# Output projection's weights split in the LRU stage, and eight of its row tiles written beside retention and GLA

## The chip, the cores and the metric

The kernel runs on one core of a Trainium2 chip, as one program with one launch. The metric is device time in microseconds (us), the median of three runs. The engines are named as in the profile: PE (TensorE, matmuls), DVE (VectorE), ACT (ScalarE), POOL (GpSimd) and SP (SyncE, which here issues nearly all DMAs). Each engine works through its own list of instructions in order, and waits at an instruction until the semaphores that it needs have come.

## The reference

One layer: four token mixers side by side on the input projection (retention, RWKV-7, RG-LRU, GLA), an output projection with a residual, and a mixture of experts in which each expert chooses its tokens. Everything is float32; the sequence has 2048 tokens of width 1024.

```python
h = _rmsnorm(x, norm_mix[l])
proj = jnp.einsum('btd,dc->btc', h, w_in[l]).astype(jnp.float32)
...
o_ret = _retention_group(rq, rk, rv, rg, positions, ret_log_decay[l], ret_gn[l])
o_rwkv = _rwkv7_group(wr, wk, wv, wxw, wxa, wxg, ...)
o_lru = _rglru_group(lx, lgate, lru_conv_w[l], ...)
o_gla = _gla_group(gq, gk, gv, gog, gxa, ...)
mixed = jnp.concatenate([o_ret, o_rwkv, o_lru, o_gla], axis=-1).astype(x.dtype)
x = x + jnp.einsum('btc,cd->btd', mixed, w_out[l])
x = x + _expert_choice_ffn(_rmsnorm(x, norm_ffn[l]), router_w[l], router_b[l], exp_w_gate[l], exp_w_up[l], exp_w_down[l])
return _rmsnorm(x, norm_final)
```

The change concerns the line with `w_out` alone: what is computed stays the same.

## The kernel before, in words

Every large matmul is done as three, on operands split into a high and a low part (`split`: ACT copies the source into the high part in a rounded format, L43, and DVE or POOL subtracts it from the source for the low part, L44; `mm3` then multiplies high by high, high by low and low by high, L129).

The program goes through these stages. (1) The input projection, with the LRU group (`lru`, once per half of its channels) written beside it: PE multiplies projections while ACT, DVE and POOL work on LRU's 128x2048 tiles. (2) The rest of the projection, beside the first half of RWKV (`stage_a`, `rwkv_a`). (3) Three streams woven by weights of their own: the second half of RWKV with what follows it (`rwkv_rest`), retention, and GLA. (4) The output projection of the row tiles that are left. (5) `top_k` of the router, and the experts.

The order of the instructions on each engine is set by a scheduler, from the order in which the program is written, the priorities of the weave, and its own estimates of time. Buffers come from pools, stacked on two sides of the on-chip memory; a pool that is closed gives its place to later ones, which then wait for the last user of that place. Two such waits matter here. LRU's pool (`lr`) gives its place to the pools of `rwkv_a`, so the first RWKV load (`ld`) waits until LRU's result (`mx<-lr_i`, L1067) has been stored. And the pools of the output projection in stage 4 (`wom`, `wo2`) lie where retention and GLA had theirs.

The output projection takes row tiles of 128 tokens. `out_weights` loads `w_out` in four pieces of 128x2048 (1 MB each) into `wo_st`, on a pool of two buffers (`wst`), and splits each into `wo_hi` and `wo_lo`; the low parts of pieces 0 and 2 are DVE's, those of 1 and 3 POOL's. `out_proj` loads the mixers' outputs of a tile from DRAM (`wo_mx<-mx`), splits them into `wo_mh` and `wo_ml`, loads the residual (`wo_x`), multiplies (48 matmuls of 128x512 for each tile), adds, and makes the router's logits. Tiles 4 to 7 (`EARLY = 4`) are written at the end of `rwkv_rest`, one tile at a time with one buffer for `wo_x`, on the right-hand pools; the other twelve, in stage 4, two at a time with two buffers.

Retention works tile by tile with one buffer for its input (`rt_ld`, L933): transposes (L938), scores (L952), outputs (L960, L963), the state's update (L909), and only then the next load. After four tiles it, as GLA, writes a block of 512 tokens to `mx` (`gated_out`, L983 to L985). SP's list holds all these loads and stores in one order.

Of the kernel before, what the change touches and what calls it, by code (L numbers as in the profile page):

```python
# [6 lines left out]
F32 = mybir.dt.float32  # L7
F32R = mybir.dt.float32r
# [9 lines left out]
P = 128  # L18
T = 2048
D = 1024  # L20
KD = D // P
# [19 lines left out]
def split(g, hi, lo, src, pool=False):  # L41

    g.nc.scalar.activation(out=hi, in_=src, func=AF.Copy)  # L43
    (g.nc.gpsimd if pool else g.nc.vector).tensor_tensor(out=lo, in0=src, in1=hi.bitcast(F32), op=OP.subtract)  # L44
# [191 lines left out]
def drain(gen):  # L236
    for _ in gen:
        pass
# [1010 lines left out]
CAP = 2 * T // NE  # L1249
HROW = D + NE  # L1250
LATE = 5
EARLY = 4
WA, WP = 84, 92
JOIN = 3
WR, WG = 100, 68
# [9 lines left out]
    c["fs_tok"] = np.stack([np.broadcast_to(np.arange(NB, dtype=f), (128, NB)), np.broadcast_to(i[:, None].astype(f), (128, NB))], 2).copy()  # L1265


def out_weights(g):
    nc, d, big = g.nc, g.d, g.wo
    whi = big.tile([P, KD, D], F32R, name="wo_hi")  # L1270
    wlo = big.tile([P, KD, D], F32R, name="wo_lo")
    nf = big.tile([P, D], F32, name="wo_nf")
    rw = big.tile([P, KD, 32], F32, name="wo_rw")
    nc.gpsimd.memset(rw, 0.0)
    g.consts(big, "fs_e")
    rb = big.tile([P, NE], F32, name="wo_rb")
    g.wout = whi, wlo, nf, rw, rb
    for n in range(4):
        st = g.wst.tile([P, KD, 256], F32, name="wo_st")
        s = slice(256 * n, 256 * n + 256)  # L1280
        nc.sync.dma_start(out=st, in_=d["w_out"][0, :, s].rearrange("(k p) c -> p k c", p=P))
        split(g, whi[:, :, s], wlo[:, :, s], st, n % 2)
        if n == 3:
            nc.sync.dma_start(out=nf, in_=d["norm_ffn"].broadcast_to([P, D]))
            nc.sync.dma_start(out=rw[:, :, 0:NE], in_=d["router_w"][0].rearrange("(k p) e -> p k e", p=P))
            nft = big.tile([P, KD], F32, name="wo_nft")
            nc.sync.dma_start(out=nft, in_=d["norm_ffn"][0].rearrange("(k p) -> p k", p=P), allow_slow_non_contiguous=True)
            nc.vector.tensor_tensor(out=rw, in0=rw, in1=nft[:, :, None].broadcast_to([P, KD, 32]), op=OP.mult)
            nc.sync.dma_start(out=rb, in_=d["router_b"].broadcast_to([P, NE]))
        yield  # L1290
# [375 lines left out]
def program(tc, d, out):  # L1666
    g = Ctx()
    g.tc, g.nc, g.d = tc, tc.nc, d
    nc = g.nc
# [11 lines left out]
    def pool(es, name, bufs, **kw):  # L1681
        return es.enter_context(tc.tile_pool(name=name, bufs=bufs, **kw))
# [9 lines left out]
    with ExitStack() as es:  # L1692
# [4 lines left out]
        dt = g.dr.tile  # L1697
# [3 lines left out]
        g.rw_tl = dt([4, 64, 1024], F32, name="rw_tl")  # L1701
        g.ysp = [dt([NB, P, 256], F32, name=f"ysp{i}") for i in range(2)]
        g.rw_dg, g.rw_ti = (dt([4, P, 1024], F32, name=n) for n in ("rw_dg", "rw_ti"))
        g.bonus = dt([P, 2, T], F32, name="bonus")
        g.gl_sp = dt([NB // GB, P, 4 * GP], F32, name="gl_sp")
        g.mx = dt([P, KD, T], F32, name="mx")
# [7 lines left out]
        with ExitStack() as es1:  # L1714
# [17 lines left out]
            with ExitStack() as es2:  # L1732
                g.lp = pool(es2, "lr", 1)
                g.stream = 0
                lru(g, 0)
                lru(g, 1)
                g.stream = 1
                drain(second)
            g.ap, g.ip = pool(es1, "ra", 1), pool(es1, "ri", 1)
# [19 lines left out]
        right = es.enter_context(ExitStack())  # L1759

        def rwkv_rest():
            g.fin = pool(right, "fin", 1, side="right")
            with ExitStack() as es1:
                g.fp, g.bp = pool(es1, "rf", 1, side="right"), pool(es1, "rb", 2, side="right")
                g.rj = pool(es1, "rj", 1, side="right")
                g.mp, g.ep = pool(es1, "rm", 4, side="right"), pool(es1, "re", 4, side="right")
                rwkv_b_buffers(g)
                yield from rwkv_b(g)
            g.wo = pool(right, "wo", 1, side="right")
            with ExitStack() as es1:  # L1770
                g.wst = pool(es1, "wst", 2, side="right")
                yield from out_weights(g)
            p1, p2 = pool(right, "we", 2, side="right"), pool(right, "we2", 1, side="right")
            yield from out_proj(g, p1, p2, range(4, 4 + EARLY), 1, 0, 1)
        with ExitStack() as es1:
            g.rp, g.rw2 = pool(es1, "rt", 1), pool(es1, "rt2", 1)
            g.gb, g.gw, g.sh = pool(es1, "gl", 1), pool(es1, "gl2", 1), pool(es1, "sh", 1)
            consts(g.rp, "rt_zt rt_inv")
            consts(g.gb, "gl_m gl_hq")
            rest = streamed(g, 0, rwkv_rest())  # L1780
            next(rest)
            g.stream = 1
            ret_tables(g)
            drain(weave((rest, WR), (streamed(g, 1, retention(g)), 56), (streamed(g, 2, gla(g)), WG)))
        g.stream = 0
        with ExitStack() as es1:
            p1, p2 = pool(es1, "wom", 2), pool(es1, "wo2", 2)
            drain(out_proj(g, p1, p2, [*range(4 + EARLY, 12, 2), 0, 2, 12, 14], 2, 1, 2))
        right.close()
# [36 lines left out]
```

## Time and profile before

| what | value |
|---|---|
| runs of the kernel before | 2861.94 us median (2858.56, 2861.94, 2866.71) |
| the profiled execution | 2858.58 us, span 2856.6 us |
| busy share of the span | PE 91%, weight loads 81%, DVE 61%, ACT 49%, POOL 25% |
| DMA | 538.40 MB, mean 188 GB/s |

The span is the time from the first to the last instruction in the profile; the execution's own time is 2.0 us longer. Times in views are us from the span's start. A row of a timeline gives start, duration, engine, line, operation, output and inputs, and in brackets the idle time of the engine just before, with what ended it.

### The profile page before, as it was taken

What the parts mean: (1) busy time and instruction counts of PE and PEld (TensorE: products, weight loads), DVE (VectorE), ACT (ScalarE), POOL (GpSimd) and SP (SyncE); (2) the same over time, 40 slices, a digit from 0 to 9 for tenths busy, and PEclk for the clock granted to TensorE, in tenths of its full rate; (3) what the DMA queues carried; (4) which work ended last, traced back from release to release, by engine and by line L of the source; (5) the groups of instructions that cost most, each with busy time, mean ns of one, the idle gap of its engine ahead of it and who ended that gap; (6) DMA issues with size and microseconds to landing.
All of it is one profiled execution on the core that took longest, in us unless ns stands there. A gap on an engine that the chain in (4) does not pass through costs nothing.

```text
span 2856.6 us, 47428 instructions
## 1 busy us (share of the span) xinstructions
PE 2594.7 (91%) x18433; PEld 2321.6 (81%) x18433; DVE 1746.1 (61%) x3415; ACT 1392.3 (49%) x2348; POOL 711.5 (25%) x771
## 2 busy tenths in 40 slices
PE   6989998989888888886979859999999999999997
PEld 5866787768767777774767659999999999999987
DVE  4454567766887667788443475555555555566564
ACT  4366555435434676555533334444444444455453
POOL 0011115443524454347433200000000000000121
PEclk9999999999988889997989979999999999999999
DMA  8735554675446544446344346666666666789873
GB/s 304 278 101 190 182 164 151 203 231 166 136 122 177 161 153 148 145 127 190 107 143 171 127 147 206 205 206 205 206 205 205 205 206 206 228 289 298 266 238 140
DMA packets 474015, 538.40 MB, mean 188 GB/s; under 512 B 129952, under 2 KB 411584, under 8 KB 473024
## 3 DMA queue, kind: packets, MB, share of 16 engines
q1 hardware_dynamic: 461984, 492.12, 53.3%
q0 software_dynamic: 11808, 43.26, 5.8%
q8 instruction: 145, 2.38, 0.3%
q14 instruction: 78, 0.64, 0.1%
HBM read 392.17 MB, written 145.23 MB: 188 GB/s over the span
## 4 chain that ended last, share of the span: by engine, by line
PE 53%; DVE 5%; DMA 4%; ACT 3%; issue 2%; POOL 1%; SPq 0%; POOLq 0%; ACTq 0%; DVEq 0%
PE bank L129 43%; DMA rt_ld<-tm 1%; PE bank L656 1%; PE bank L1500 1%; PE bank L639 1%; DMA fn_x<-acc,x_idx 1%; PE bank L628 1%; PE bank L672 1%; PE bank L1481 1%; PE bank L648 1%; DVE tk_j L1395 0%; PE bank L1217 0%; PE bank L1323 0%; PE bank L960 0%; PE bank L952 0%
## 5 line engine op out<-in xcount | busy, mean ns | idle before, releaser
L44 DVE TENSOR_TENSOR x_wl<-x_st,x_wh 128x2048 fp32r<-128x2048 f32 x192 | 439.5, 2292 | 306.3 <-ACT x_wh L43 305.9
L129 PE MATMUL bank<-x_xh,x_wh 128*128 128x256 f32 x2048 | 580.2, 285 | 2.9 <-ACT x_wh L43 2.8
L129 PE MATMUL bank<-x_xl,x_wh 128*128 128x256 f32 x2048 | 577.4, 283 | 0.0
L129 PE MATMUL bank<-x_xh,x_wl 128*128 128x256 f32 x2048 | 572.2, 283 | 1.1 <-DVE x_wl L44 1.1
L43 ACT ACTIVATE x_wh<-x_st 128x2048 fp32r<-128x2048 f32 x192 | 367.0, 1913 | 106.7 <-PE bank L129 96.6
L129 PEld LDWEIGHTS bank<-x_xh,x_wh 128*128 128x128 f32 x2048 | 393.2, 192 | 3.6 <-ACT x_wh L43 3.2
L129 PEld LDWEIGHTS bank<-x_xl,x_wh 128*128 128x128 f32 x2048 | 393.3, 192 | 0.0
L129 PEld LDWEIGHTS bank<-x_xh,x_wl 128*128 128x128 f32 x2048 | 389.9, 192 | 1.5 <-DVE x_wl L44 1.5
L129 PE MATMUL bank<-x_wh,x_hh 128*128 128x256 f32 x1024 | 290.1, 285 | 4.8 <-ACT x_hh L43 4.8
L129 PE MATMUL bank<-x_wl,x_hh 128*128 128x256 f32 x1024 | 291.2, 285 | 0.0
L129 PE MATMUL bank<-x_wh,x_hl 128*128 128x256 f32 x1024 | 289.8, 284 | 0.0
L1626 POOL DMA_INDIRECT acc<-x_os,x_idx x30 | 48.9, 1631 | 926.8 <-ACT x_os L1560 899.0
L129 PE MATMUL bank<-h_hi,w_hi 128*128 128x512 f32 x576 | 238.5, 417 | 20.1 <-DVE o_cm L1676 13.8
L129 PE MATMUL bank<-h_lo,w_hi 128*128 128x512 f32 x576 | 240.0, 417 | 0.0
L129 PE MATMUL bank<-h_hi,w_lo 128*128 128x512 f32 x576 | 235.6, 409 | 0.0
L129 PEld LDWEIGHTS bank<-x_wh,x_hh 128*128 128x128 f32 x1024 | 196.6, 193 | 5.0 <-ACT x_hh L43 5.0
L129 PEld LDWEIGHTS bank<-x_wl,x_hh 128*128 128x128 f32 x1024 | 197.4, 193 | 0.0
L129 PEld LDWEIGHTS bank<-x_wh,x_hl 128*128 128x128 f32 x1024 | 197.2, 193 | 0.0
L129 PE MATMUL bank<-w_hi,h_hi 128*128 128x256 f32 (+1 forms) x512 | 156.4, 306 | 14.6 <-DVE o_tm L1676 11.8
L129 PEld LDWEIGHTS bank<-h_hi,w_hi 128*128 128x128 f32 x576 | 112.5, 196 | 56.3 <-DVE o_cm L1676 16.4
L129 PE MATMUL bank<-w_lo,h_hi 128*128 128x256 f32 (+1 forms) x512 | 149.4, 292 | 0.0
L129 PE MATMUL bank<-w_hi,h_lo 128*128 128x256 f32 (+1 forms) x512 | 148.8, 291 | 0.0
(457 smaller groups left out, 5490.2 us busy)
## 6 DMA issues: line engine op xcount, KB each, us to landing
x_st<-in_exp_w_gate_dram SPq DMA_DIRECT2D x64, 1024.0 KB, 8.4
x_st<-in_exp_w_up_dram SPq DMA_DIRECT2D x64, 1024.0 KB, 8.9
x_st<-in_exp_w_down_dram SPq DMA_DIRECT2D x64, 1024.0 KB, 5.5
w_st<-in_w_in_dram SPq DMA_DIRECT2D x20, 1024.0 KB, 6.7
rw_sp<-sp SPq DMA_DIRECT2D x16, 1280.0 KB, 4.6
bld<-rw_sp SPq DMA_DIRECT2D x32, 640.0 KB, 4.1
ld<-rw_cm SPq DMA_DIRECT2D x14, 899.5 KB, 6.1
cm<-o_cm SPq DMA_DIRECT2D x40, 256.0 KB, 2.8
```

The lines of the kernel that those rows point to most:

```text
L43: g.nc.scalar.activation(out=hi, in_=src, func=AF.Copy)
L44: (g.nc.gpsimd if pool else g.nc.vector).tensor_tensor(out=lo, in0=src, in1=hi.bitcast(F32), op=OP.subtract)
L129: g.nc.tensor.matmul(out, lhsT=lhs[a][:, k, lsl], rhs=rhs[b][:, k, rsl], start=(k + i == 0 and out is outs[0]), stop=(3 * k + i == 3 * nk ...
L628: nc.tensor.matmul(pss[k][:, q * P:(q + 1) * P], lhsT=z[q][H[k]], rhs=ks, start=True, stop=True)
L639: nc.tensor.matmul(ps[:, o:o + P], lhsT=bk[q][e], rhs=rd[:, 2 * q + 1 - e], start=True, stop=True)
L648: nc.tensor.matmul(ps[:, h * P:(h + 1) * P], lhsT=ti[:, h], rhs=R[:, h], start=True, stop=True)
L656: nc.tensor.matmul(ps[:, h * 256:(h + 1) * 256], lhsT=X[:, 2 * h2 + h, :], rhs=q0[:, 2 * h2 + h].rearrange("p e c -> p (e c)"), start=True ...
L672: nc.tensor.matmul(ps[:, h, :], lhsT=E[:, h, e, :], rhs=mv[e][:, h, :], start=True, stop=True)
L1481: nc.tensor.matmul(ps[:, 2 * s:2 * s + 2], lhsT=oh[:, i, s * P:(s + 1) * P], rhs=tok[:, i], start=(i == 0), stop=(i == NB - 1))
L1500: nc.tensor.transpose(ps[:, m * CAP + s * P:m * CAP + (s + 1) * P], xs[:, s, (k + m) * P:(k + m + 1) * P], c["ident"])
L1626: g.nc.gpsimd.indirect_dma_start(out=dst, out_offset=bass.IndirectOffsetOnAxis(ap=idx[:, s:s + 1], axis=0), in_=t[:, s], in_offset=None, **kw)
```

## The change

Three edits. A new function, `out_split`, stands behind the two calls of `lru`, in their pool: in 16 pieces of 128x512 it loads `w_out`, splits each piece (ACT for the high part, DVE for the low part) and stores both parts in two new DRAM tensors, `wo_sp`. Its buffers (`wo_st`, `wo_sh`, `wo_sl`) are one of each. `out_weights` no longer splits: it loads the two parts from there, eight loads of 1 MB straight into `wo_hi` and `wo_lo`, and the pool `wst` is gone. `EARLY` goes from 4 to 8: tiles 4 to 11 are written in `rwkv_rest`, and stage 4 keeps tiles 0 to 3 and 12 to 15.

```diff
-EARLY = 4
+EARLY = 8
...
+def out_split(g):
+
+    nc = g.nc
+    for n in range(4):
+        for k in range(0, KD, 2):
+            st = g.lp.tile([P, 2, 256], F32, name="wo_st", tag="wo_st")
+            hi = g.lp.tile([P, 2, 256], F32R, name="wo_sh", tag="wo_sh")
+            lo = g.lp.tile([P, 2, 256], F32R, name="wo_sl", tag="wo_sl")
+            s = slice(256 * n, 256 * n + 256)
+            nc.sync.dma_start(out=st, in_=g.d["w_out"][0, k * P:(k + 2) * P, s].rearrange("(k p) c -> p k c", p=P))
+            split(g, hi, lo, st)
+            for t, o in zip((hi, lo), g.wo_sp):
+                nc.sync.dma_start(out=o[:, k:k + 2, s], in_=t.bitcast(F32))
...
     for n in range(4):
-        st = g.wst.tile([P, KD, 256], F32, name="wo_st")
         s = slice(256 * n, 256 * n + 256)
-        nc.sync.dma_start(out=st, in_=d["w_out"][0, :, s].rearrange("(k p) c -> p k c", p=P))
-        split(g, whi[:, :, s], wlo[:, :, s], st, n % 2)
+        for t, k in zip((whi, wlo), g.wo_sp):
+            nc.sync.dma_start(out=t[:, :, s].bitcast(F32), in_=k[:, :, s])
...
+        g.wo_sp = [dt([P, KD, D], F32, name=f"wo_sp{i}") for i in range(2)]
...
                 lru(g, 1)
+                out_split(g)
                 g.stream = 1
                 drain(second)
...
-            with ExitStack() as es1:
-                g.wst = pool(es1, "wst", 2, side="right")
-                yield from out_weights(g)
+            yield from out_weights(g)
             p1, p2 = pool(right, "we", 2, side="right"), pool(right, "we2", 1, side="right")
             yield from out_proj(g, p1, p2, range(4, 4 + EARLY), 1, 0, 1)
```

Lines of the changed kernel are 14 higher behind `out_split` (L1301 is L1315, L1309 is L1323, L1678 is L1692), and 14 to 16 lines higher further on. The scheduler's order is the same on PE from early in `rwkv_a` until shortly after RWKV's last chain; it differs in the LRU stage and behind that point.

ACT in the first half of LRU, before: sigmoids (`lr_r`, `lr_i`), a square (`lr_a`), a square root (`lr_th`), and the table loads between them.

```order
L1046 ACTIVATE lr_i<-bank,lr_gb 128x512
L1052 ACTIVATE lr_a_1133<-lr_r 128x2048
L1046 ACTIVATE lr_i<-bank,lr_gb 128x512 x2
L1046 ACTIVATE lr_r<-bank,lr_gb 128x512
L1055 ACT_TABLE_LOAD
L1055 ACTIVATE lr_th<-lr_th 128x2048
L1046 ACT_TABLE_LOAD
L1046 ACTIVATE lr_r<-bank,lr_gb 128x512 x3
```

The same place in the changed kernel:

```order
L1046 ACTIVATE lr_i<-bank,lr_gb 128x512
L43 ACTIVATE wo_sh<-wo_st 128x512
L1046 ACTIVATE lr_i<-bank,lr_gb 128x512 x2
L1052 ACTIVATE lr_a_1135<-lr_r 128x2048
L1046 ACTIVATE lr_i<-bank,lr_gb 128x512
L43 ACTIVATE wo_sh<-wo_st 128x512
L1046 ACTIVATE lr_r<-bank,lr_gb 128x512
L1055 ACT_TABLE_LOAD
L1055 ACTIVATE lr_th<-lr_th 128x2048
L1046 ACT_TABLE_LOAD
L1046 ACTIVATE lr_r<-bank,lr_gb 128x512 x2
L43 ACTIVATE wo_sh<-wo_st 128x512
```

Three of the sixteen high parts (`wo_sh`) now stand between LRU's instructions here. In all, six stand in the first half's run of sigmoids and square roots, which has one table load fewer than before, and four in the second half's; the other six stand between these runs or ahead of them.

SP behind RWKV's last chain, before: the last two loads of `w_out` (`wo_st`), then RWKV's, GLA's and retention's loads, and the first tile's `wo_mx`.

```order
L1281 DMA wo_st<-in_w_out_dram 128x8x256
L764 DMA rw_y_12854<-ysp_76 128x2x256
L769 DMA bon<-bonus 128x2x256
L1146 DMA gl_p<-gl_sp 128x1024
L1281 DMA wo_st<-in_w_out_dram 128x8x256
L1181 DMA gl_v<-tm 128x2x256
L764 DMA rw_y_12853<-ysp_75 128x2x256
L767 DMA xg<-rw_cm 128x256
L785 DMA mx<-bon 128x2x256
L1301 DMA wo_mx<-mx 128x8x128
L933 DMA rt_ld<-tm 128x768
```

The changed kernel, the end of the eight loads of the split weights (six more stand right ahead of these rows, and one retention load, of tile A below, ahead of those):

```order
L1296 DMA wo_hi<-wo_sp_79 128x8x256
L764 DMA rw_y_12936<-ysp_75 128x2x256
L1296 DMA wo_lo<-wo_sp_80 128x8x256
L767 DMA xg<-rw_cm 128x256
L1298 DMA wo_nf<-in_norm_ffn_dram 128x1024
L785 DMA mx<-bon 128x2x256
L1299 DMA wo_rw<-in_router_w_dram 128x8x16
L1301 DMA wo_nft<-in_norm_ffn_dram 128x8x1
L1303 DMA wo_rb<-in_router_b_dram 128x16
L1315 DMA wo_mx<-mx 128x8x128
L1146 DMA gl_p<-gl_sp 128x1024
L933 DMA rt_ld<-tm 128x768
```

The next retention load (of tile B), GLA's `gl_p` and RWKV's `rw_y` now stand behind 8 MB of weights.

PE at its first matmul of the output projection, before: GLA, the gate of a retention block (L983), RWKV's output (L778, L780), and then the projection.

```order
L1217 MATMUL bank<-gl_qx,gl_p 128x512
L1236 MATMUL bank<-gl_v,gl_sT 128x64 x4
L1217 MATMUL bank<-gl_qx,gl_p 128x512
L1233 MATMUL bank<-gl_sx_7412,gl_p 128x256
L1234 MATMUL bank<-gl_sx_7413,gl_p 128x256
L983 MATMUL bank<-c_ident,rt_y_10496 128x128 x8
L778 MATMUL bank<-c_ident,rw_y_12853 128x128 x4
L780 MATMUL bank<-xg,rw_g_up 128x256 x2
L129 MATMUL bank<-wo_hi,wo_mh 128x512
L129 MATMUL bank<-wo_lo,wo_mh 128x512
```

The changed kernel, from the end of retention's tile B (its last output and its state's update) to the first matmul of the projection:

```order
L960 MATMUL bank<-rt_sd_7497,rt_qs 128x128
L963 MATMUL bank<-rt_ld,rt_sT 128x64 x2
L909 MATMUL bank<-rt_ld,rt_kz 128x128 x2
L938 MATMUL bank<-c_ident,rt_a_11758 128x128 x4
L1153 MATMUL bank<-c_ident,gl_p 128x128 x2
L952 MATMUL bank<-rt_qd_7493,rt_kT 128x256 x2
L778 MATMUL bank<-c_ident,rw_y_12983 128x128 x4
L780 MATMUL bank<-xg,rw_g_up 128x256 x2
L129 MATMUL bank<-wo_hi,wo_mh 128x512
L129 MATMUL bank<-wo_lo,wo_mh 128x512
```

Ahead of the first projection matmul PE now does all of retention's tile B and the front (L938, L952) of tile C, where it had done tile A alone: 36 more matmuls (16 of tile B, 6 of tile C, GLA's 8 gate transposes, 6 small ones). At the far end, matmuls of stage 4's tiles 0 to 3 now stand between those of tiles 6 to 11, ahead of the last block of retention and GLA.

## Rows read from the trace of the kernel before

**Rows 1.** The chain that ended last, in order of time: start, us, what, count.
```profile
1446.03 9.23 DMA wo_mx<-mx
1465.29 7.68 PE bank L129 x24
1473.85 5.62 PE bank L129 x24
1627.52 2.85 DMA c_fs_iota<-in_c_fs_iota_dram
```

**Rows 2.** Windows: us; busy PE, PEld, DVE, ACT, POOL; PE clock; DMA share; GB/s.
```profile
1300.00:1350.00 50.00, 25.70 (x107) 17.60 (x107) 45.01 (x75) 25.84 (x53) 41.49 (x33) 0.66 0.50 151
1350.00:1450.00 100.00, 91.15 (x532) 72.71 (x530) 48.34 (x131) 46.82 (x109) 48.00 (x46) 0.94 0.34 114
1450.00:1475.00 25.00, 11.65 (x46) 9.48 (x47) 12.30 (x31) 7.75 (x9) 9.41 (x5) 0.61 0.47 153
1475.00:1525.00 50.00, 50.00 (x272) 39.01 (x271) 19.73 (x63) 19.23 (x34) 17.55 (x10) 1.00 0.48 170
```

**Rows 3.** Timeline of DVE and POOL, the splits of the weights.
```profile
1301.02 10.27 DVE L44 TENSOR_TENSOR wo_lo<-wo_st,wo_hi 128x2048 fp32r<-128x2048 f32 x1 [0.79 <-ACT wo_hi L43]
1320.05 2.29 DVE L44 TENSOR_TENSOR wo_lo<-wo_st,wo_hi 128x2048 fp32r<-128x2048 f32 x1
1324.40 4.61 POOL L44 TENSOR_TENSOR wo_lo<-wo_st,wo_hi 128x2048 fp32r<-128x2048 f32 x1 [0.52 <-ACT wo_hi L43]
```

**Rows 4.** Waits of PE between 1290 and 1480: us, times, longest.
```profile
PE bank L1233 <- DVE gl_t L1227: 8.2, 1, 8.2
```

**Rows 5.** Timeline of SP, loads and stores issued (start, us of issue).
```profile
1288.01 1.17 SPq L1281 DMA_DIRECT2D wo_st<-in_w_out_dram  x2
1293.48 0.52 SPq L933 DMA_DIRECT2D rt_ld<-tm  x1
1329.50 0.53 SPq L1301 DMA_DIRECT2D wo_mx<-mx  x1
```

**Rows 6.** DMAs of 1284 to 1335 (GB/s in 40 slices), and `wo_x` there and in 1380 to 1440.
```profile
GB/s 265 219 240 43 258 364 376 341 353 381 409 410 226 285 288 242 335 95 6 1 0 0 158 372 376 366 357 371 355 139 180 0 0 6 107 202 258 257 377 238
wo_x<-in_x_dram SPq DMA_DIRECT2D x1, 512.0 KB, 8.1
wo_x<-in_x_dram SPq DMA_DIRECT2D x3, 512.0 KB, 3.6
```

**Rows 7.** Timeline of SP and PE, one retention tile, and the first projection matmul.
```profile
1275.91 0.32 SPq L933 DMA_DIRECT2D rt_ld<-tm  x1
1287.32 1.10 PE L952 MATMUL bank<-rt_qd,rt_kT 128*128 128x256 f32 x4
1290.59 0.66 PE L909 MATMUL bank<-rt_ld,rt_kz 128*128 128x128 f32 x4
1352.82 0.80 PE L129 MATMUL bank<-wo_hi,wo_mh 128*128 128x512 f32 x1
```

**Rows 8.** Timeline of POOL, ACT and PE where LRU ends and `rwkv_a` begins.
```profile
288.31 1.81 POOL L1741 MEMSET bl<- 128x2048 f32 x1 [16.19 <-DMA mx<-lr_i]
297.09 0.42 ACT L356 ACTIVATE xwa<-xwa 64x256 f32<-64x256 f32 x1
299.92 1.14 PE L362 MATMUL bank<-xwa,rw_up 64*128 64x256 f32 x8
```

**Rows 9.** Rows nearest to a 128x512 piece: one tile's groups (ns), timelines (us).
```profile
L43 ACT ACTIVATE wo_mh<-wo_mx x20: 612/1040/1064, 1334.0 to 1573.4; 128x1024 fp32r<-128x1024 f32 x12, 128x512 fp32r<-128x512 f32 x8
1280.86 0.68 DVE L878 TENSOR_TENSOR rt_a<-rt_ld,rt_cs 128x512 f32<-128x512 f32 x1
168.81 1.28 ACT L1055 ACT_TABLE_LOAD   x1
252.75 2.29 DVE L1056 TENSOR_TENSOR lr_i<-lr_i,lr_th 128x2048 f32<-128x2048 f32 x1 [3.87 <-POOL lr_i L1047]
DMA to landing us min/median/max: 2.6/2.7/2.9
```

## The prediction

> **What bounds the kernel now.** I read the chain of waits in order of time first. From the experts on it is PE's matmuls without a break, so what counts is when the top-k begins: the chain meets its first load at 1627.5 [rows 1]. Ahead of that the chain enters stage 4 through a load of `mx` at 1446.0, and PE's first matmul of that stage comes at 1465.3 [rows 1]. The windows over this stretch come next. From 1475 on PE is busy all the time; in 1450 to 1475 it is busy 11.65 of 25 us, in 1350 to 1450 91.15 of 100, in 1300 to 1350 25.70 of 50 [rows 2]. So PE is the bound, with three holes of 24.3, 8.85 and 13.35 us, and the change can win what it fills of these.
>
> The first hole lies where the weights are split. DVE spends 10.27 us on one low part and 2.29 on an equal one; POOL takes 4.61 for its own [rows 3]. PE meanwhile waits 8.2 us for a GLA instruction that DVE has behind the split [rows 4]. The third hole is a change of pools: tile 8's load can only be issued when retention and GLA have left their place, and nothing else is written for PE there.
>
> **The change part by part.** The sum is made on the profiled execution: span 2856.6, own time 2858.58, which is 3.4 below the median of 2861.94.
>
> *The third hole.* By the changed order, matmuls of tiles 0 to 3 and 6 to 11 stand around the end of retention and GLA, all on weights and buffers that are there by then. PE has work while stage 4's pools change: 13.35 us go. After the hole the first 24 matmuls took 7.68 us where the next 24 took 5.62 [rows 1], and the granted clock in that window was 0.61, in the next 1.00 [rows 2]; without the idle time I take these 2.1 us as won too. Together 15.4.
>
> *The first hole, the weights.* What goes from DVE, ACT and POOL are four splits (DVE 12.6 us, POOL about 9.2 [rows 3]). What comes is a load of 8.4 MB in place of 4.2 MB. The slices of 1.3 us in which the old loads ran (the fifth to the twelfth that hold 258 to 410) have a mean of about 361 GB/s [rows 6], so 8.4 MB need 23 us. In the changed order the eight loads stand behind retention's load for tile A, which was issued at 1293.5 [rows 5], and some small transfers; I put their first byte at about 1298 and their last at 1322. The first tile's `wo_mx` is queued right behind them, where it was issued at 1329.5 before [rows 5]: the weights themselves come a few us earlier than now.
>
> That does not help PE at once, since its order now holds retention's tile B and the front of tile C ahead of the first projection matmul. Retention has one input buffer. An undisturbed tile took from the load's issue at 1275.9 to the end of L909 at 1291.25, 15.3 us, and reached L952 after 11.4 [rows 7]. So tile A ends at 1293.5 + 15.3 = 1309. Tile B's load is issued then, but stands behind the weights, `wo_mx` and `gl_p` (1 MB more, 3 us): it lands at about 1326, where it would have landed near 1313 on an empty queue, and tile B ends at 1326 + 12 = 1338. Tile C's load comes at about 1340, its L952 at 1351, and the first projection matmul at about 1353. It is at 1352.8 now [rows 7]: no gain, no loss. The gain is what PE has done by then: 36 more matmuls. Tile B from L952 to L909 is 3.9 us [rows 7]; with the transposes and the GLA gate I count 7 us for all 36. They fill a part of the first hole.
>
> *The second hole.* Tiles 4 to 7 are woven with retention and GLA as now, one tile at a time on one `wo_x` buffer. I leave the 8.85 us as they are, though the order differs; the bounds are nothing (8.85 won) and twice as much (8.85 lost, if eight tiles on one buffer stall more than four).
>
> *The LRU stage.* 16 pieces come in, each with a load, a copy on ACT, a subtraction on DVE and two stores. The nearest rows: 0.61 us for an ACT copy of 128x512, 0.68 for a DVE operation of that size on two on-chip inputs, 2.6 to 2.9 us for a 256 KB load to land [rows 9]. The DMAs (12.6 MB, 35 us at 361 GB/s) find room in a stage of 170 us; no row shows them beside this traffic, so zero is the lower bound and the pieces' own latency the upper one, below. ACT has ten copies within LRU's dense runs: 6.1 us, less one table load of 1.28 [rows 9]. On DVE most subtractions fall where it idles for POOL's product, 3.87 us in the row shown [rows 9]; two do not, 1.4. LRU's end is thus 6.2 us later, and it is what `rwkv_a` waits for: POOL's clearing of `bl` started on the landing of `mx<-lr_i` [rows 8]. PE reached L362 2.4 us after its input was ready (297.5 and 299.92 [rows 8]), and the changed order puts L362 three matmuls later, 1.2 us. Of 6.2 us some 2.6 are left, and I take 3 for the loss. From there on PE's order is as before, so a shift of 3 us is carried to the end.
>
> *SP's list.* SP waits in order. Stores of a piece stand between stores of projection results, so a late ACT copy holds those stores; PE goes on as long as the two result buffers last. I put that at 0, with the cover of one buffer (some 10 us of matmuls).
>
> *Sum.* -15.4 - 7 + 3 = -19.4. Own time 2858.6 - 19.4 = 2839; against the median 2842.5. **Forecast: 2843.**
>
> **A rule on the queue.** The 512 KB load of `wo_x` took 8.1 us to land behind the 2 MB of `wo_st`, and 3.6 later on, so transfers queued on SP's list wait for those ahead [rows 6]. The Trainium skill (DMA: Bandwidth & Descriptors, Queues, rings and completion order) says that descriptors of a queue are taken in ring order and that a transfer's semaphore write lands only after every earlier write of that DMA engine. By that rule every load of retention, GLA and RWKV behind the eight is held for their whole drain, and the trace agrees as far as these two rows go. What it gives here is rival A: the price is set by the drain, from rows.
>
> **The rivals.**
>
> *A: the 8.4 MB hold retention back, and the gain is used up.* The 361 GB/s above are those of a burst; over 1300 to 1350 only 151 GB/s were moved, and over all 40 slices about 230 [rows 2, 6]. At 230 GB/s the 8.4 MB take 36.5 us instead of 23, and the 1 MB behind them 4.5 instead of 3: tile B comes 15 us later, and so does the first projection matmul. For it: PE's order puts tiles B and C ahead of that. Against it: the low slices are those in which nothing was asked for. The gain shrinks from 22.4 to about 7, the result to -4: 2858, no difference. Chance 0.17.
>
> *B: slower, through LRU.* If each of the ten copies in LRU's runs stands at ACT's head waiting for its load, a piece costs 2.7 us to land, 0.61, and 0.68 before the buffer is free [rows 9]: 4.0 times ten is 40 us on LRU's end, with 3.6 of slack and order. The loss is 36, the sum +14: 2876. It decides against the change once LRU ends more than 26 us later (22.4 + 3.6). For it: one buffer per piece, a load behind SP's waits, ACT and PE coupled through LRU's banks. Against it: in the changed order several LRU instructions stand between two copies on ACT, 5 to 8 us by their durations, more than a load takes. Chance 0.10.
>
> *C: more of the holes is filled.* If tile B's load lands early, so that the projection starts at 1340, and half of the second hole goes as well, 13 + 4.4 us more: 2825. The first hole is 24.3 us wide, and DVE is free in it now. Chance 0.13.
>
> **How the numbers follow.** Forecast 0.60, A 0.17, B 0.10, C 0.13. The forecast's own bounds: the second hole gone or doubled (8.85 either way) and LRU's loss between 0 and 8, so 2831 to 2857. For 8 in 10 I take 2828 to 2862, which adds A and the near part of C. A change under 0.3% (8.6 us) is about what three runs of this kernel, 8 us apart, can't tell from none. Faster by more (below 2853.4): 0.73, most of the forecast and C, with a little of A. Within 0.3%: 0.17. Slower: 0.10, rival B.
>
> **What would show it right or wrong.** In the changed profile: the DVE and POOL splits of 128x2048 of `wo_st` are gone, and eight loads of `wo_hi` and `wo_lo` are issued within a few us near 1298. The first projection matmul comes at about 1356 (1353 and 3 of shift), with PE still half idle before it; behind it there is no window like 1450 to 1475, and the top-k's first load is issued at about 1608. `mx<-lr_i` of the second half lands some 6 us later, and L362 starts near 303. The prediction is wrong if LRU's end moves by more than 15 us, if tile B's load lands after 1335, or if PE idles behind the first projection matmul, for instance on the single `wo_x` buffer or because its list has a retention matmul, not yet ready, ahead of projection matmuls that are.

## The result, and the profile after

The change is slower: 2885.12 us median of 6 runs (2877.14 to 2890.19), against 2867.05 for the kernel before in the same session (6 runs, 2858.56 to 2871.09); ratio 1.0065, 95% interval 1.0049 to 1.0080, some 18 us. The forecast was 2843, with a range to 2862. The profiled executions stand further apart (spans 2883.7 and 2856.6), because the one of before took 2858.58, as long as the fastest of its six. So totals below go by ratios of medians, and profiles serve to find places. In rows, SPq and ACTq are DMAs that SP or ACT issues.

Timeline of SP in the changed kernel: retention's load of tile A, part of the loads behind it, tile B's and tile C's loads, and the first of the top-k's loads (start, us of issue):

```profile
1321.38 0.46 SPq L933 DMA_DIRECT2D rt_ld<-tm  x1
...
1322.84 0.52 SPq L1296 DMA_DIRECT2D wo_hi<-wo_sp  x1
1323.42 0.75 SPq L1296 DMA_DIRECT2D wo_lo<-wo_sp  x1
1324.20 2.93 SPq L1296 DMA_DIRECT2D wo_hi<-wo_sp  x1
1327.18 3.14 SPq L1296 DMA_DIRECT2D wo_lo<-wo_sp  x1
...
1342.49 0.72 SPq L1296 DMA_DIRECT2D wo_lo<-wo_sp  x1
...
1350.57 3.58 SPq L1303 DMA_DIRECT2D wo_rb<-in_router_b_dram  x1
...
1355.52 0.38 SPq L933 DMA_DIRECT2D rt_ld<-tm  x1
...
1382.10 0.32 SPq L933 DMA_DIRECT2D rt_ld<-tm  x1
...
1652.27 0.33 SPq L1702 DMA_DIRECT2D c_fs_sum<-in_c_fs_sum_dram  x1
```

The load of the top-k before:

```profile
1626.18 0.33 SPq L1688 DMA_DIRECT2D c_fs_sum<-in_c_fs_sum_dram  x1
```

Tile A's load stood at 1293.48 before [rows 5] and stands 27.9 us later: in this pair of profiles that much is lost ahead of the part that the change is about. From there to `c_fs_sum` it is 330.9 us; before it was 332.7. So behind tile A 1.8 us are won, where the forecast had 22.4.

Timeline of PE in the changed kernel, two places at which it had waited, the end of tile B (L909) between them, and the first projection matmul:

```profile
1368.20 1.11 PE L778 MATMUL bank<-c_ident,rw_y 128*128 128x128 f32 x4 [9.03 <-DVE rw_y L81]
...
1380.86 1.17 PE L909 MATMUL bank<-rt_ld,rt_kz 128*128 128x128 f32 x4
...
1388.51 1.12 PE L938 MATMUL bank<-c_ident,rt_a 128*128 128x128 f32 x4 [6.48 <-POOL rt_a L880]
...
1395.64 0.99 PE L129 MATMUL bank<-wo_hi,wo_mh 128*128 128x512 f32 x1
```

Windows (columns as in [rows 2]), from tile A's load to the first projection matmul and from there to `c_fs_sum`, first of the kernel before and then of the changed kernel, which has two more rows:

```profile
1293.48:1352.82 59.34, 34.16 (x132) 23.36 (x133) 53.31 (x95) 30.45 (x64) 46.66 (x38) 0.66 0.56 174
1352.82:1626.18 273.36, 251.16 (x1401) 195.51 (x1400) 113.02 (x354) 105.55 (x213) 103.26 (x77) 0.95 0.39 136
```

```profile
1321.38:1395.64 74.26, 44.92 (x186) 32.11 (x187) 53.60 (x115) 29.81 (x76) 41.50 (x44) 0.69 0.75 236
1395.64:1652.27 256.63, 241.63 (x1347) 189.24 (x1346) 108.03 (x332) 96.74 (x199) 99.13 (x74) 0.98 0.40 133
1359.20:1368.20 9.00, 0.00 (x0) 0.00 (x0) 8.46 (x27) 2.85 (x5) 4.78 (x5) 0.72 0.88 300
1525.00:1600.00 75.00, 67.86 (x388) 52.04 (x387) 22.90 (x91) 21.33 (x48) 16.55 (x14) 0.98 0.31 108
```

The first projection matmul comes 74.3 us behind tile A's load, where it came after 59.3 [rows 5, 7]. Of the 15 us more, 10.8 are PE's own busy time (34.16 before, 44.92 now) and 4.2 are idle time (25.18 before, 29.34 now). In the longest wait, 9.03 us ahead of 1368.20, DVE is busy for 8.46 of 9 us.

Behind the first projection matmul PE idles 15.00 us, where it had idled 22.20. The third hole is PE's wait ahead of L983, the gate of a retention block, before and in the changed kernel:

```profile
1463.27 1.94 PE L983 MATMUL bank<-c_ident,rt_y 128*128 128x128 f32 x8 [16.04 <-DVE hn_t L59]
```

```profile
1463.69 1.97 PE L983 MATMUL bank<-c_ident,rt_y 128*128 128x128 f32 x8 [6.03 <-DVE rt_y L81]
```

It shrinks by 10 us. The rest of the idle time grows from 6.2 to 9.0, of which 7.14 stand in 1525 to 1600, where PE had been busy all the time before.

The rows that answer to [rows 8], the end of LRU:

```profile
292.49 0.32 SPq L1067 DMA_DIRECT2D mx<-lr_i  x1
301.08 0.37 SPq L315 DMA_DIRECT2D ld<-rw_cm  x1
301.43 1.81 POOL L1757 MEMSET bl<- 128x2048 f32 x1 [21.28 <-DMA rw_cm<-o_cm]
310.24 1.14 PE L362 MATMUL bank<-xwa,rw_up 64*128 64x256 f32 x8 [3.45 <-ACT xwa L356]
```

The first two of them before:

```profile
284.05 0.32 SPq L1067 DMA_DIRECT2D mx<-lr_i  x1
...
288.89 0.38 SPq L315 DMA_DIRECT2D ld<-rw_cm  x1
```

LRU's result is stored 8.4 us later, the next stage's first load comes 12.2 later and L362 10.3 later, now waiting for its input.

### The profile page after: what moved, and what is told of

Read it like the earlier page. It is cut to its first block, busy times and chain, and to the rows that moved or that the text cites. A ratio compares the mean times of both kernels' runs of the same rounds, so it can differ in the third digit from the quotient of the medians.

```text
span 2883.7 us, 47582 instructions
## 1 busy us (share of the span) xinstructions
PE 2604.0 (90%) x18433; PEld 2328.5 (81%) x18433; DVE 1764.2 (61%) x3429; ACT 1391.8 (48%) x2363; POOL 701.6 (24%) x773
## 4 chain that ended last, share of the span: by engine, by line
PE 57%; DVE 14%; DMA 11%; ACT 8%; issue 5%; POOL 2%; SPq 1%; POOLq 0%; DVEq 0%; ACTq 0%
PE bank L129 46%; DMA ld<-rw_cm 3%; PE bank L639 1%; DVE x L485 1%; PE bank L656 1%; DMA wo_st<-in_w_out_dram 1%; PE bank L1514 1%; DMA fn_x<-acc,x_idx 1%; POOL pr L484 1%; DMA rt_ld<-tm 1%; PE bank L672 1%; DMA xt<-in_x_dram 1%; PE bank L648 1%; PE bank L628 1%; DVE pr L484 1%
## 5 line engine op out<-in xcount | busy, mean ns | idle before, releaser
L129 PE MATMUL bank<-w_hi,h_hi 128*128 128x256 f32 (+1 forms) x512 | 157.2, 307 | 14.2 <-DVE o_tm L1690 11.5
```

The lines of the kernel that those rows point to most:

```text
L129: g.nc.tensor.matmul(out, lhsT=lhs[a][:, k, lsl], rhs=rhs[b][:, k, rsl], start=(k + i == 0 and out is outs[0]), stop=(3 * k + i == 3 * nk ...
```

## The experiments

Three places were open: the LRU stage (theories 1 and 1a to 1d), the first hole (3 to 3d, and 4), and the early tiles (2 to 2c). "Shift at 350" is the median, over instructions matched by line and names, of how much later than before those run that started between 350 and 375 us before. The last two columns are us from tile A's load to the first projection matmul and to `c_fs_sum`, in each profile. These are single profiles: the five kernels with the change's work behind LRU (the change, one_piece8, lru_stores, lru_noload, lru_two) differ by 6.4 us in the last column.

| kernel | ratio to before | 95% interval | shift at 350 | projection | top-k |
|---|---|---|---|---|---|
| before | 1 | | 0 | 59.3 | 332.7 |
| the change | 1.0065 | 1.0049–1.0080 | 16.0 | 74.3 | 330.9 |
| early4 | 1.0019 | 1.0004–1.0033 | 13.5 | 71.5 | 318.3 |
| early6 | 1.0031 | 1.0014–1.0048 | 13.1 | 70.8 | 325.5 |
| early8_only | 0.9994 | 0.9979–1.0009 | -0.8 | 61.5 | 327.6 |
| one_piece8 | 1.0006 | 0.9990–1.0022 | 1.0 | 74.4 | 332.8 |
| lru_stores | 1.0021 | 1.0003–1.0040 | 5.2 | 74.5 | 332.6 |
| lru_noload | 1.0036 | 1.0024–1.0048 | 8.4 | 70.6 | 326.4 |
| lru_two | 1.0046 | 1.0031–1.0061 | 11.5 | 71.9 | 330.4 |
| lru_pool4 | 0.9993 | 0.9980–1.0005 | 13.6 | 71.8 | 319.9 |
| stage_a4 | 1.0038 | 1.0025–1.0051 | 1.1 | 70.4 | 317.7 |
| two_x | 1.0060 | 1.0041–1.0079 | 14.2 | 65.5 | 334.4 |
| act_queue | 1.0111 | 1.0085–1.0137 | 15.8 | 87.4 | 348.7 |
| hi_only | 1.0061 | 1.0039–1.0084 | 12.9 | 73.2 | 332.5 |
| pool_low | 0.9984 | 0.9974–0.9995 | -1.4 | 57.6 | 328.5 |
| pool_low6 | 0.9959 | 0.9936–0.9981 | -1.8 | 60.7 | 324.6 |
| pool_low8 | 0.9984 | 0.9969–0.9998 | -0.9 | 57.3 | 324.0 |

### The change taken apart

**early4**: `EARLY = 4` in the changed kernel.

> The change with EARLY = 4: weights split in the LRU stage and loaded split, but tiles 4 to 7 alone beside retention and GLA. PE's order is that of the change up to where tile 8 begins. Theory 1 (the time lost is lost in two places that the early tiles do not touch, some 16 us in the LRU stage, grown to 25 by 1280, and some 17 us in the first hole, where the loads of the split weights keep SP's list): first projection matmul at about 1395 as in the change, hole at the change of pools back at about 13 us, result about 2857 + 25 + 17 = 2900, ratio to before about 1.014. Rival (the eight early tiles are what stalls, on one wo_x buffer): time back to about 2865, ratio about 1.00.

13 us better than the change. Theory 1's ratio is far off and the rival's is near, but neither has the whole: the losses of LRU and of the first hole are there, as theory 1 has it, and the tail is 318.3 us, 14.4 shorter than before.

**early8_only**: `EARLY = 8` in the kernel before.

> The kernel before with EARLY = 8 alone; the weights are split on the chip as before. PE's order is that of before up to the end of tile 7's matmuls. Theory 1 (early tiles fill the hole at the change of pools, some 13 us, and lose 7 to 11 again where the last early tiles run alone on one wo_x buffer): 2 to 8 us faster, ratio 0.997 to 0.999, no idle time in 1450 to 1475 and about 7 us of new idle time before the top-k. My forecast's own terms (15 us, nothing lost): ratio 0.995. Rival (single wo_x buffer costs more than the hole): slower, ratio 1.003 or more.

No difference that can be told; the tail is 5.1 us shorter in the profile, as theory 1 has it, though PE still idles 6.63 us in 1450 to 1475, where theory 1 had none. The early tiles win little by themselves. On top of the split weights they lose: 330.9 against 318.3, of which 9.8 us lie behind the first projection matmul.

### The LRU stage

**one_piece8**: out of the LRU stage with it; one piece is split, and stored everywhere.

```diff
-                out_split(g)
...
+                    if i == 0:
+                        parts = out_piece(g, g.ap, 0)
+                    for q in (2 * i, 2 * i + 1):
+                        out_store(g, parts, q)
```

> The change with the LRU stage as before: one piece of 128x256 is loaded and split once, in a pool of the second stage, and its two parts are stored 32 times (8.4 MB, spread over the second stage), so the projection multiplies by wrong weights. PE's order is that of before up to the end of LRU and that of the change from the loads of the split weights on. Theory 1 (the pieces between LRU's instructions cost 11 to 16 us at LRU's end and about 20 by 1275; the tail of the change gains 2): ratio to before 0.998 to 1.002, first RWKV load at 289, from retention's load of tile A to the top-k 331 us as in the change. Rival (the 8.4 MB of stores or the drift after LRU cost the time): ratio 1.004 or more.

Theory 1 holds: 1.0065 falls to 1.0006. The pieces in the LRU stage, with all that follows from them, cost 0.59%, 17 us (some 6 either way by the two intervals), and the rest of the change nets nothing (332.8 us behind tile A).

**lru_stores** moves the load and `split` out of the loop over the 16 places and keeps the 32 stores in it; **lru_noload** moves only the load out; **lru_two** keeps everything, with a second buffer:

```diff
-            st = g.lp.tile([P, 2, 256], F32, name="wo_st", tag="wo_st")
+            st = g.lp.tile([P, 2, 256], F32R, name="wo_st", tag="wo_st", bufs=2)
...
-            split(g, hi, lo, st)
+            split(g, hi, st, st.bitcast(F32))
```

> The change with one piece loaded and split in the LRU stage, and its two parts stored into all 16 places (32 stores of 256 KB, all still in the LRU stage's part of SP's list); the projection multiplies by wrong weights. PE's order from the second stage on is that of the change. Theory 1c (the stores, on the queues and in SP's list, are the price of the LRU stage): ratio to before 1.005 to 1.007, as the change. Rival (ACT's copies and DVE's subtractions, and their waits, are the price): shift at 350 under 5 us, ratio 0.999 to 1.002.

> The change with 16 copies, 16 subtractions and 32 stores in the LRU stage, all from one piece that is loaded once (wrong weights). Theory 1a (ACT stands at a copy until its load has landed, 24 us in 8 waits): shift at 350 falls from 13 to 16 us to under 6, ratio 1.000 to 1.002. Rival 1d (copies, subtractions and one buffer for each part, which is free only when its store has landed): shift 10 us or more, ratio 1.004 or more.

> The change with two buffers for a piece's load, the low part written in place of the loaded piece; 16 pieces, same engines. PE's order behind the LRU stage is that of the change. Theory 1a (ACT stands at a piece's copy until its load has landed, 24 us in 8 waits, and LRU's sigmoids stand behind it): with the next load under way, the shift at the first RWKV load falls from 12 to 5 us or less, result about 2872. Rival 1b (the work itself, the slow subtractions on DVE beside POOL, and SP's list between the stores): shift stays at 10 us or more, result 2882 to 2888.

None of the single causes carries it: lru_stores comes out just above its rival's 5 us, lru_noload between its two cases, lru_two between them in the ratio (the shift at the first RWKV load is 16.3 us, as rival 1b has it). From one_piece8 through lru_stores and lru_noload to the change the shift at 350 climbs 1.0, 5.2, 8.4, 14.3 (mean of the change, early4, early6, two_x, act_queue and hi_only, which share this stage), the ratios 1.0006, 1.0021, 1.0036, 1.0065: about 4 us for the stores, 3 to 4 for copies and subtractions, 6 to 8 for the loads, of which a second buffer gives back 3 to 5. Most intervals overlap from one step to the next, and each run has its own order of ACT's instructions in this stage, so the shares are rough. Waits of ACT in 110 to 300 (total, times, longest), in the change, lru_noload and lru_two:

```profile
ACT wo_sh L43 <- DMA wo_st<-in_w_out_dram: 24.2, 8, 6.0
```

```profile
ACT wo_sh L43 <- DVE wo_sl L44: 17.6, 7, 4.4
```

```profile
ACT wo_sh L43 <- DMA wo_sp<-wo_sh: 22.7, 5, 8.9
```

In the change ACT waits for loads that had not landed. Take the loads away and it waits for DVE's subtraction; give them a second buffer and it waits for the store of `wo_sh`, which has one buffer still. So lru_two moved the wait more than it removed it, and no run here has two buffers for all parts. LRU's sigmoids and copies of projections stand behind these waits. Waits of PE for ACT's copies of projections in 110 to 375, in the change and before:

```profile
PE bank L129 <- ACT o_cm L1692: 9.2, 4, 4.4
```

```profile
PE bank L129 <- ACT o_cm L1678: 0.6, 1, 0.6
```

Those for DVE's copies fall meanwhile, from 9.9 to 4.3. All waits of PE in that stretch grow from 15.3 to 27.4 us: 3.0 for copies of projections, 3.9 at LRU's gates (L1045) and 3.5 at L362 are the largest parts.

Timeline of POOL, and of DVE, in the change:

```profile
165.81 6.10 POOL L1047 TENSOR_TENSOR lr_i<-lr_i,lr_xc 128x2048 f32<-128x2048 f32 x1 [53.41 <-ACT lr_i L1046]
```

```profile
162.22 0.69 DVE L44 TENSOR_TENSOR wo_sl<-wo_st,wo_sh 128x512 fp32r<-128x512 f32 x1 [9.68 <-ACT wo_sh L43]
...
167.42 5.04 DVE L44 TENSOR_TENSOR wo_sl<-wo_st,wo_sh 128x512 fp32r<-128x512 f32 x1
172.38 2.28 DVE L1056 TENSOR_TENSOR lr_i<-lr_i,lr_th 128x2048 f32<-128x2048 f32 x1
```

The same product and what follows it on DVE, before:

```profile
168.30 5.54 POOL L1047 TENSOR_TENSOR lr_i<-lr_i,lr_xc 128x2048 f32<-128x2048 f32 x1 [54.20 <-ACT lr_i L1046]
```

```profile
173.87 2.29 DVE L1056 TENSOR_TENSOR lr_i<-lr_i,lr_th 128x2048 f32<-128x2048 f32 x1 [4.48 <-POOL lr_i L1047]
```

DVE's 0.69 us subtraction takes 5.04 beside POOL's product. But it fills a wait of 4.48 us that DVE had there before. L1056 starts 0.5 us after the product's end, where it had started at once, and the product takes 6.10 us in place of 5.54. So on DVE's own list the place that I had called free cost about 1 us here, and three subtractions stand in such places. What it costs that a slow subtraction frees its buffers late, no run shows by itself.

**lru_pool4**: lru_two with `EARLY = 4` and the subtraction on POOL.

> The change with EARLY = 4, two buffers for a piece's load, and the low part subtracted in place by POOL, not by DVE. Output complete. PE's order from the second stage on is that of the change with EARLY = 4. Theory 1 (LRU's price falls to 8 us or less with the load ahead and no slow subtraction on DVE, and four early tiles on weights loaded split win 14): ratio 0.996 to 0.999. Rival (POOL's products for LRU now stand behind subtractions that wait for ACT's copies, and LRU ends later by as much as in the change): ratio 1.002 or more.

Between the two: the tail wins 12.8 and the LRU stage still costs 13.6 (theory 1 had 8 or less), no difference.

**stage_a4**: two half-size pieces behind each tile of the second stage, `EARLY = 4`.

> Two pieces of 128x256 loaded, split (ACT, DVE) and stored behind each of the 16 tiles of the second stage, in place of the 16 pieces in the LRU stage, and EARLY = 4. Output complete. Theory 1: nothing lost in the LRU stage, 318 us from tile A's load to the top-k as with four early tiles and the weights loaded split (333 before), so 14 us won, less what 32 small subtractions on DVE, 11 us in a stage where DVE is busy 70%, lose: ratio 0.995 to 0.999. Rival (DVE's and ACT's order in the second stage holds PE as it did in LRU): ratio 1.002 or more.

The LRU stage is free of loss (1.1) and the tail short (317.7), but the second stage loses 24 us between 350 and 550. Waits of PE in 350 to 805, of stage_a4 and then of the kernel before:

```profile
PE bank L129 <- DVE o_tm L1691: 23.2, 13, 4.4
PE bank L423 <- POOL pc L420: 14.1, 7, 3.5
```

```profile
PE bank L129 <- DVE o_tm L1676: 15.0, 10, 2.9
...
PE bank L423 <- POOL pc L420: 5.6, 3, 3.3
```

**one_piece**, one_piece8 with its piece in the pool `ca`, settled nothing: LRU's first load came at 123.8 in place of 113.5, and everything was 34 us late at 100, ahead of all that it was to tell. Probably the two tiles moved LRU's pool; no run shows it. Ratio 1.0125 (1.0109 to 1.0142).

> The change without its splits in the LRU stage: one piece of 128x256 is split once, and its two parts are stored 32 times, into all places of the two DRAM tensors, during the second stage (so the projection multiplies by wrong weights; all transfers and later work are there). Theory 1 (the pieces in the LRU stage cost 16 us there and what grows out of it): first RWKV load at about 289, retention's load of tile A at about 1297 in place of 1321, result about 25 us under the change, 2860, ratio about 1.00. Rival (the loss comes from 8.4 MB of stores on the queues, wherever they stand, or from the reserved buffers): still over 2878.

### The first hole

**act_queue**: `nc.scalar.dma_start` for the eight loads.

> The change with the eight loads of the split weights issued by ACT, not by SP. Theory 3 (SP's list is what holds retention: each of the eight issues takes 2.8 us there once the queue is full, and tile B's load stands behind them): tile B's load is issued within 20 us of tile A's in place of 34, the first projection matmul comes 60 us after tile A's load in place of 74. Rival 3b (the drain itself, 316 GB/s in that stretch, delays every other load whoever issues it): first projection matmul still 70 us or more behind tile A's load, result as the change.

It is worse than the change, as neither case had it: ACT now stood at the issues, and tile B's load came 40.0 us behind tile A's. So theory 3's condition was not met, and the next run is the better test. Timeline of ACT in act_queue:

```profile
1315.47 3.97 ACTq L1296 DMA_DIRECT2D wo_hi<-wo_sp  x1
...
1319.47 4.80 ACTq L1296 DMA_DIRECT2D wo_lo<-wo_sp  x1
1324.32 0.38 ACT L1225 ACTIVATE gl_sT<-bank 64x256 f32<-64x256 f32 x1 [8.19 <-issue]
```

The Trainium skill (DMA: Bandwidth & Descriptors, Issuing engines are not separate DMA queues) says that DMAs of all issuers run on the same 16 engines, so another issuer only saves issue time, which is usually small. The trace agrees with the first half: while the eight loads of ACT and the transfers of SP drain together, most slices of 1 us hold about 350 GB/s, as they do in the change, where SP issues all. The issues, at 3.97 and 4.80 us, were not small here.

**hi_only**: no loads of `wo_lo`; `wo_hi` is multiplied in its place.

> The change with only the four loads of the high parts; wo_hi stands in for wo_lo in the products (so the projection has wrong low terms). 4.2 MB in place of 8.4 MB come at the place where tile B's load waits; PE's first projection matmul stands at the same place of its order. Theory 3c (SP stands while the queue drains, 2.8 us a load of 1 MB, and tile B's load, rw_y and wo_mx stand behind it): four loads less bring tile B's load about 12 us earlier (20 to 24 us behind tile A's in place of 34) and the first projection matmul to 60 to 64 us behind tile A's load in place of 74; ratio to before 1.001 to 1.004. Rival 3d (PE's order and DVE's norms hold it, whatever is loaded): first projection matmul still 70 us or more behind tile A's load, ratio as the change.

This run decides, against 3c. Timelines of SP, POOL and PE in hi_only:

```profile
1318.54 0.42 SPq L933 DMA_DIRECT2D rt_ld<-tm  x1
...
1340.93 0.39 SPq L933 DMA_DIRECT2D rt_ld<-tm  x1
```

```profile
1358.89 1.25 POOL L880 TENSOR_TENSOR rt_a<-rt_a,rt_a 128x512 f32<-128x512 f32 x1
```

```profile
1365.53 0.66 PE L778 MATMUL bank<-c_ident,rw_y 128*128 128x128 f32 x4 [2.27 <-DVE rw_y L81]
1367.59 1.06 PE L938 MATMUL bank<-c_ident,rt_a 128*128 128x128 f32 x4
...
1391.72 0.81 PE L129 MATMUL bank<-wo_hi,wo_mh 128*128 128x512 f32 x2
```

Tile B's load is issued 22.4 us behind tile A's, as theory 3c wants, but PE comes to tile B (L938 at 1367.59) 26.7 us after that, and to the projection 73.2 after tile A's load, as in the change. POOL had tile B ready for L938 at 1360.14; PE reached it 7.5 us later, behind GLA's matmuls and RWKV's L778, for which it waited until DVE was through. With half the bytes nothing is won. So what stands ahead in PE's order, and the small operations on DVE and POOL that PE waits for, are what is left to hold it; no run has the eight loads with the order of before.

**pool_low**: the kernel before with `split(..., st, True)`, every low part on POOL.

> The kernel before with all four low parts of the output projection's weights split by POOL, none by DVE; nothing else is changed. It relieves DVE of what the change relieves it of, without a load more and without the LRU stage. Theory 4 (PE's wait of 8.2 us in the first hole is that for a GLA instruction behind DVE's split): first hole shorter by 5 to 8 us, ratio 0.997 to 0.998. Rival 4b (POOL, with 18 us of splits in place of 9, holds retention and GLA as long, and the weights are ready later): ratio 1.000 or more.

0.16% faster, clear of one but small. The hole did not shrink as theory 4 has it: PE idles 31.3 us between tile A's load and the first projection matmul (25.2 before), which comes 1.7 us earlier.

### The early tiles

**two_x**: two `wo_x`, one `wo_ml` for early tiles. **early6**: `EARLY = 6` in the change. **pool_low6**, **pool_low8**: pool_low with `EARLY` 6 and 8.

> The change with two buffers for the early tiles' wo_x, and one for wo_ml to make the room. Theory 2 (the last early tiles run alone on one wo_x buffer, which a tile holds until its normed rows are stored; PE idles some 8 us there): idle time of PE behind the first projection matmul falls from 15.6 to under 10 us, from tile A's load to the top-k 320 to 324 us in place of 331, result about 2877, ratio to before 1.003. Rival (the order in which the early tiles are written, not the buffer, is what leaves PE idle, or the single wo_ml stalls as much): 328 us or more, ratio still 1.006.

> The change with EARLY = 6 (tiles 4 to 9 beside retention and GLA). PE's order is that of the change until its last early tiles. Theory 2b (from tile A's load to the top-k, 318 us with four early tiles and 331 with eight: each tile that is written early beyond those that have retention or GLA beside them shows its own chain of add, transposes, copies and logits, 2 to 3 us a tile): 322 to 326 us, ratio 1.003 to 1.005, two such bare tiles in place of four. Rival 2c (a fixed loss as soon as tiles beyond 7 stand beside stage 4's, whatever their number): 329 us or more, ratio 1.006.

> The kernel before with all four low parts on POOL and EARLY = 6; nothing split ahead. Theory 2b: the hole at the change of pools (14 us with four early tiles) halves, and two bare tiles cost 4 to 6: ratio 0.995 to 0.998. Rival 2c: 0.998 to 1.000, no better than with four.

> The kernel before with all four low parts on POOL and EARLY = 8; nothing split ahead. Theory 2b: the hole at the change of pools goes (14 us) and four bare tiles cost 8 to 12: ratio 0.996 to 0.999. Rival 2c: 0.999 or more, the early tiles win nothing here either.

two_x is a miss: no gain (idle time behind the first projection matmul 20.6, the change 15.0), though its single `wo_ml` may hide one. early6 lies between: 318.3, 325.5, 330.9 us for 4, 6 and 8 tiles, as theory 2b has it. But part of this lies ahead of the first projection matmul, which early tiles don't touch. Behind it (the last column of the table less the one before) the three take 246.8, 254.8 and 256.6 us, and PE idles 6.9, 15.0 and 15.0 of them. That is nearer to rival 2c, a fixed loss. That eight tiles cost more than four there, about 10 us, is clear: early4, lru_pool4 and stage_a4 take 246.8 to 248.1, the five kernels with the change's tail 255.8 to 258.5. How it is shared among the tiles is open. The chain of one tile that nothing fills, in PE's timeline of the change, has four short waits, 1.6 us in all:

```profile
1560.73 1.25 PE L1337 MATMUL bank<-c_ident,wo_x 128*128 128x128 f32 x8 [0.64 <-DVE wo_x L1327]
1562.17 0.43 PE L1342 MATMUL bank<-wo_hT,wo_rw 128*32 128x128 f32 x8 [0.19 <-DVE wo_hT L1690]
1562.99 0.43 PE L1342 MATMUL bank<-wo_hT,wo_rw 128*32 128x128 f32 x8 [0.39 <-ACT wo_hT L1692]
1563.81 0.39 PE L1346 MATMUL bank<-c_fs_e,wo_lt 128*128 128x16 f32 x2 [0.40 <-ACT wo_lt L1344]
```

By the changed order, matmuls of tiles 0 to 3, which could have filled such waits, stand ahead of this place. pool_low6 has the best ratio of all and beats both kernels, 0.41% faster than before; its interval overlaps those of pool_low and pool_low8, which are at 0.9984 both, so what the six early tiles add is not shown. Its windows:

```profile
1300.00:1350.00 50.00, 21.20 (x78) 13.77 (x78) 36.98 (x58) 21.30 (x41) 35.54 (x25) 0.64 0.56 170
...
1450.00:1475.00 25.00, 21.21 (x123) 17.13 (x122) 19.72 (x52) 11.01 (x18) 11.37 (x7) 1.00 0.59 201
1475.00:1525.00 50.00, 46.23 (x248) 36.06 (x247) 22.52 (x66) 20.08 (x32) 16.32 (x10) 0.97 0.41 145
```

Its first hole is wider than before (28.80 us of idle PE in the first window, 24.30 before [rows 2]); the gain is in 1450 to 1475 (3.79 idle, 13.35 before), of which 3.77 are lost again in the next window.

## Why the prediction was wrong, point by point

**The LRU stage, +3: mis-sized, and the largest error.** Measured 17 us by medians. LRU's end did move by about what I had counted (6.0 to 8.4 us in the six kernels with this stage, against 6.2). Wrong was that slack and order would take half of it back: L362 waited for its input, where it had been ready 2.4 us early, and by 350 the shift is 14.3. I had looked for the cost in LRU's end only. Yet lru_two's LRU ends 17.2 us late, later than the change's, and its shift at 350 is smaller. The term for SP's list, put at 0 because PE goes on while the result buffers last, was wrong too: PE's waits up to 375 grow by 12 us, at copies of projections, at LRU's gates and at L362. I had set the DMAs' cost at nothing; stores alone take about 4 us, waits for loads more. Rival B had ACT's waits (24.2 us in eight), but not the path: LRU's end did not move by its 36 to 40.

**The first hole, no gain and no loss: the step that failed.** It was that tile B ends 12 us after its load lands, that the first projection matmul comes at 1353, and that the 36 matmuls put ahead of it fill idle time of PE. The matmul comes 15.0 us later, relative to tile A. From tile C's load on the forecast held (13.5 us to the matmul, forecast 13); the time is lost by the end of tile B, 60.7 us behind tile A's load, where I had 44.5. The 36 matmuls (54 records in the trace) lengthen PE's busy time by 10.8 us, where I had 7, and PE's idle time is 4.2 longer, where I had it 7 shorter. So they were paid for, not found. The drain itself went near the forecast (issues of 1 MB came at a pace of about 345 GB/s; the forecast had 361), though SP stood at them; that tile B's load would stand behind it was right too. But hi_only shows that neither sets the matmul. I had taken one retention tile's undisturbed time [rows 7]; here PE's order has GLA's and RWKV's steps between, each waiting for DVE or POOL. Rival A gives the right loss (15 us) by a mechanism that hi_only does not bear out.

**Behind the first projection matmul, -22.4.** Measured -16.8 in the change (273.4 to 256.6 us: 9.5 of busy and 7.2 of idle PE) and -26.6 with four early tiles. The third hole does not go: its 16.04 us become 6.03, and new idle time in the last tiles gives 2.8 back. I had read the holes from windows with an edge at 1450: 2.8 us of what I called the second hole belong to the third. I had named the single `wo_x` as what would stall; two_x does not bear that out.

**The sum**: +17, +15.0 and -16.8 make +15; measured is +18. What separates the two lies within the intervals. The forecast had A and B exclude each other; a loss of A's size and half of B's came together, and either alone would have left the change near or below before.

**Of the signs I had named**, the splits are gone and `mx<-lr_i` is late as said; LRU's end stays under the 15 us that I had set. The loads took 20 us to issue, tile B's load was issued at 1355.5, past the 1335 that I had set, PE idles behind the first projection matmul, and the top-k begins at 1652 and not at 1608.

**Left open**: which chain of the first hole is the longest, how the early tiles' loss is shared, what two buffers for every part of a piece would give back, and whether the drift of the change's profile between 350 and 1275 (16.0 to 25.7) is more than scatter: tile A's load stands between 1303.5 and 1321.4 in six kernels with the same LRU stage.

## What to carry to other kernels

That engines idle in a stage does not make work free that is moved there: price it by what it holds up on each engine's list, and try it with the work left out, as one_piece8 does. If the order puts more work ahead of a matmul, do not count on it to fill the idle time there: that work costs its latency in the present pace of that stretch, not its duration in a quiet one. When a wait is taken away from an instruction, look at what it waits for next. Tiles written early won something here only while other streams filled the waits of their tails.

## What the runs showed of the hardware

In the change an issue of a 1 MB load took 0.52 and 0.75 us for the first two, 2.93 and 3.14 for the next two, and one of 8 KB took 3.58. At 1.05 MB each the pace of those two is about 345 GB/s, near the 361 of [rows 6]: the issues went as fast as the transfers. The issuing engine stands meanwhile (ACT 8.19 us in act_queue). In the LRU stage a DVE subtraction of two on-chip inputs took 5.04 us in place of 0.69 beside a POOL product: it started 1.6 us after the product's start and ended 0.55 after its end. The Trainium skill (GPSIMD Engine Reference, Specifications) says that POOL's memory interfaces contend with DVE instructions of two such inputs; the rows agree.
